# Loading the first slices of weights and of x through one queue in a forced order, in a two-layer hybrid decoder trunk

## The chip, the cores and the metric

The kernel runs on one core of one Trainium2 chip. The metric is the device time of one execution in microseconds; for the kernel before it is the median of three runs. The engines are named as in the profile: PE multiplies matrices (PEld is its weight load), DVE, ACT and POOL are the vector, scalar and GpSimd engines, SP only issues transfers here. ACT has a transfer queue of its own too (ACTq beside SPq in the rows).

## The reference

Two layers, each of them one projection of x (512 tokens by 1024) to 3352 columns, three mixers on slices of those columns, an output projection, and a layer norm:

```python
def hybrid_layer(x, w_in, w_out, ...):
    proj = x @ w_in
    (rq, rk, rv, rg, nq, nkc, nvc, nks, nvs, nkw, nvw, ng, ngl, lx, lg) = jnp.split(proj, IN_SPLIT_POINTS, axis=-1)
    y_ret = retention(rq, rk, rv) * jax.nn.silu(rg)
    y_nsa = nsa(nq, nkc, nvc, nks, nvs, nkw, nvw, ngl, cmp_pos, cmp_w) * jax.nn.silu(ng)
    y_lru = rg_lru(lx, conv_w, conv_b, w_a, b_a, w_x, b_x, lam) * jax.nn.silu(lg)
    y = jnp.concatenate([y_ret, y_nsa, y_lru], axis=-1) @ w_out
    return layer_norm(DEEPNORM_ALPHA * x + y, ln_g, ln_b)
```

`retention` is a chunked decayed attention of 4 heads, `nsa` an attention of 8 query heads with a compressed, a selected and a window branch, `rg_lru` a gated linear recurrence behind a short convolution.

## The kernel before

**Products.** The contraction over 1024 is cut into 8 slices of 128, called k0 to k7. Each operand is split into a rounded high part and a low rest (`wh` and `wl` of the weights, `XH` and `XL` of x), and each k takes three products, high by high, high by low and low by high, which add up in one PSUM bank. The banks are A (three: A_96, A_97, A_98 in the rows of the program), S (two: S_99, S_100), and T, M and O (one each).

**Weights.** The columns of w_in come in chunks of 256 (the first, `nv`, has 280), in the order nv, nk, nq0, cmp, nq1 and so on. A chunk is loaded in two halves of four k each (h0 is k0 to k3, h1 is k4 to k7). A half goes from HBM into one of **two** raw buffers `wr` (wr_86, wr_87), ACT rounds it into one of four `wh` (wh_88 to wh_91), and POOL, in some cases DVE, subtracts into one of four `wl` (wl_92 to wl_95). The next half can be fetched into a raw buffer only when its last `wl` piece has been made. Only the chunk nv of the first layer is different: its two halves, and x itself, come in eight transfers each, one for each k (`load_x` issues the one for x). ACT then makes `XH` and DVE `XL`. In the rows x is written to a buffer named Y, since it borrows a stage of that name.

**The first products.** nv takes 96 products of 280 columns (four tiles of 128 tokens, 8 k, three products), two of its tiles in banks A and two in banks S. nk, nq0 and the later chunks take 48 products of 512 columns each. K, Q and Y are what ACT and DVE copy out of the banks for the attention of nk, nq0 and cmp.

**Order.** The code does not run in the order in which it is written. Every call on an engine is recorded as an `Op` in a `Plan`; `schedule` lists all operations by priorities from their costs (with a little seeded noise), forward and backward six times, and `emit` issues them, engine by engine, in the order of their planned starts. The queue of SP is planned in the same way, as an engine. An engine runs its own list in order, so that an instruction that waits holds up those behind it. A change in the first operations can so change the order of everything behind them.

**Zeros.** `WARM = 9` products of a tile of zeros with itself are recorded into bank T ahead of everything; nothing reads them as a result. `COLD` doubles the planned cost of products that are planned before 6.8 us.

Of the kernel before, what the change touches and what calls it, by code (L numbers as in the profile page):

```python
# [115 lines left out]
BANKS = dict(A=3, M=1, S=2, T=1, O=1)  # L116
PBUFS = 7
WARM = 9
W_ACT = 2

NORM = [["AG", "AG", "VV", "VV"], ["AG", "AG", "VV", "VV"]]
LOCKS = True
# [164 lines left out]
class Plan:  # L287
    ENGINES = ("PE", "DVE", "ACT", "POOL", "SP")

    def __init__(self, nc):  # L290
        self.ops, self.cells, self.bias = [], {}, 0.0
        queues = (nc.tensor, nc.vector, nc.scalar, nc.gpsimd, nc.sync)
        self.engines = [Engine(self, e, q) for e, q in zip(self.ENGINES, queues)]

# [16 lines left out]

    def add(self, eng, call, cost, reads, writes, table, lock, dma=False):
        op = Op(eng, call, cost, table, lock and LOCKS, len(self.ops))
        op.dma = dma
        for r in reads:
            q, m = self.touched(r)
            op.after.update(o for o, q2, m2 in r.buf.writes if q & q2 and m & m2)
        for r in writes:
            q, m = self.touched(r)
            op.after.update(o for o, q2, m2 in r.buf.writes + r.buf.reads if q & q2 and m & m2)  # L320
        for r in reads:
            r.buf.reads.append((op, *self.touched(r)))
        for r in writes:
            b, (q, m) = r.buf, self.touched(r)
            b.writes = [w for w in b.writes if w[1] & ~q or w[2] & ~m] + [(op, q, m)]
            b.reads = [w for w in b.reads if w[0] is op or w[1] & ~q or w[2] & ~m]
        op.after.discard(op)
        op.bufs = {r.buf for r in reads + writes}

        op.rows = {}  # L330
        if eng in ("ACT", "DVE") and not dma:
            for kind, refs in (("W", writes[:1]), ("R", reads)):
                for r in refs:
                    ap = r.view(0)
                    op.rows.setdefault((kind, ap.space == PSUM), ap.offset // ap.ap[0][0])
        for b in op.bufs:
            b.users += 1
        for o in op.after:
            o.before.append(op)
        op.bias = self.bias  # L340
        self.ops.append(op)
# [31 lines left out]
    def forward(self, prio):  # L373

        for b in {b for op in self.ops for b in op.bufs}:
            b.pool.next, b.pool.free = 0, [(0.0, s) for s in range(len(b.pool.slots))]
            b.slot, b.last, b.left, b.seen = None, 0.0, b.users, {}
        for op in self.ops:
            op.wait, op.known = len(op.after), 0.0
        ready = {e: [] for e in self.ENGINES}  # L380
        free = dict.fromkeys(self.ENGINES, BEGIN)

        table, ports = "exp", {"POOL": 0.0, "DVE": 0.0}
        rows = {"ACT": {}, "DVE": {}}
        for op in self.ops:
            if not op.wait:
                ready[op.eng].append(op)
        self.order = []

        def place(op):  # L390

            t = 0.0
            for b in op.bufs:
                if b.slot is None:
                    if b.pool.next != b.at or not b.pool.free:
                        return None
                    t = max(t, min(b.pool.free)[0])
                t = max([t] + [end + TURN for e, end in b.seen.items() if e != op.eng])
            return t

        while len(self.order) < len(self.ops):
            best = None
            for e in ("POOL", "PE", "DVE", "ACT", "SP"):
                pick = None
                for op in ready[e]:
                    at = place(op)
                    if at is None:
                        continue
                    t = max(op.known, at, free[e] + self.held(op, rows), ports[e] if op.lock else 0.0)
                    k = (t, prio[op], op.ix)  # L410
                    if pick is None or k < pick[0]:
                        pick = k, op
                if pick and (best is None or pick[0][0] < best[0][0]):
                    best = pick
            t, op = best[0][0], best[1]
            cost = op.cost
            if op.table and op.table != table:
                cost, table = cost + 1280.0, op.table
            if op.eng == "PE" and t < COLD:
                cost *= 2.0  # L420
            if op.rows:
                rows[op.eng].update(op.rows)
            for b in op.bufs:
                if b.slot is None:
                    _, b.slot = spot = min(b.pool.free)
                    b.pool.free.remove(spot)
                    b.pool.next += 1
            op.start, op.end = t, t + cost
            free[op.eng] = op.end
            if op.lock and op.eng == "POOL":  # L430
                ports["DVE"] = op.end - POOL_EARLY
            elif op.lock:
                ports["POOL"] = op.end
            ready[op.eng].remove(op)
            self.order.append(op)
            for b in op.bufs:
                b.last = max(b.last, op.end + self.release(op))
                if b.pool.turns and op.eng != "PE":
                    b.seen[op.eng] = op.end
                b.left -= 1  # L440
                if not b.left:
                    b.pool.free.append((b.last, b.slot))
            for o in op.before:
                o.wait -= 1
                o.known = max(o.known, op.end + self.lag(op, o))
                if not o.wait:
                    ready[o.eng].append(o)
        return max(op.end for op in self.order)
# [51 lines left out]
def hybrid_kernel(ctx: ExitStack, tc: tile.TileContext, xt_d, xn_d, w_in_d, w_out_d, gb_d, cmpw_d, cmpp_d, lruw_d,  # L500
                  lrup_d, const_d, out_d):
    nc = tc.nc
    plan = Plan(nc)
    T, V, A, G, Q = plan.engines
# [58 lines left out]
    def weights(l, name):  # L563
        if (l, name) not in parts:
            cl, cname, src, n = chunks[len(parts)]
            assert (cl, cname) == (l, name), (l, name)
            s3 = src.rearrange("p (k n) -> p k n", k=KT)
            first = len(parts) == 0
            got = {}
            for h in W_HALVES:  # L570
                r = slice(4 * h, 4 * h + 4)
# [2 lines left out]
                lo = sb([P, 4, 280], "wl", WBUFS, F32R)[:, :, :n]  # L574
                if first:

                    for k in range(4):
                        u = slice(k, k + 1)
                        (A if 4 * h + k < W_ACT else Q).dma_start(raw[:, u, :], s3[:, r, :][:, u, :])
                        load_x(slice(4 * h + k, 4 * h + k + 1))  # L580
                        A.activation(hi[:, u], raw[:, u], AF.Copy)
                        (G if k % 2 else V).tensor_sub(lo[:, u], raw[:, u], hi.bitcast(F32)[:, u])
                else:
                    Q.dma_start(raw, s3[:, r, :])
                    for q in range(2):
                        u = slice(2 * q, 2 * q + 2)
                        A.activation(hi[:, u], raw[:, u], AF.Copy)
                        for v in range(2 * q, 2 * q + 2, 2 // W_CUT):
                            u = slice(v, v + 2 // W_CUT)
                            (G if W_ENG[2 * h + q] == "G" else V).tensor_sub(lo[:, u], raw[:, u], hi.bitcast(F32)[:, u])  # L590
                got[h] = (hi, lo)
            parts[(l, name)] = [(got[k // 4][0][:, k % 4, :], got[k // 4][1][:, k % 4, :]) for k in range(KT)]
        return parts[(l, name)]

# [591 lines left out]
```

## Time and profile before

| | us |
|---|---|
| median of 3 runs | 577.59 (577.09 to 577.8) |
| the profiled execution, its own time | 577.81 |
| its span, first to last instruction | 576.0 |
| PE busy | 559.9 (97% of the span) |
| DVE, ACT, POOL busy | 373.8, 331.6, 336.5 |

The profile is that of one execution. Its own time is 1.8 us more than its span, which lies around the first and the last instruction. An engine counts as busy while one of its instructions runs. Spans of PE are modelled at their ends (products overlap), so the distance from start to start says what one product costs.

### The profile page before, as it was taken

What the parts mean: (1) busy time and instruction counts of PE and PEld (TensorE: products, weight loads), DVE (VectorE), ACT (ScalarE), POOL (GpSimd) and SP (SyncE); (2) the same over time, 40 slices, a digit from 0 to 9 for tenths busy, and PEclk for the clock granted to TensorE, in tenths of its full rate; (3) what the DMA queues carried; (4) which work ended last, traced back from release to release, by engine and by line L of the source; (5) the groups of instructions that cost most, each with busy time, mean ns of one, the idle gap of its engine ahead of it and who ended that gap; (6) DMA issues with size and microseconds to landing.
All of it is one profiled execution on the core that took longest, in us unless ns stands there. A gap on an engine that the chain in (4) does not pass through costs nothing.

```text
span 576.0 us, 10627 instructions
## 1 busy us (share of the span) xinstructions
PE 559.9 (97%) x3718; PEld 500.6 (87%) x3718; DVE 373.8 (65%) x1113; ACT 331.6 (58%) x754; POOL 336.5 (58%) x512
## 2 busy tenths in 40 slices
PE   8999999999999999999989999999999999999994
PEld 7877888889998988899978788888988989889993
DVE  5660378898998754632873026877898886356257
ACT  6453578897775635611535238778967564454230
POOL 3753394377956348844763447633898273478442
PEclk8999999999999999999999999999999999999998
DMA  8743233020323036244253434211122122352303
GB/s 280 243 125 93 77 93 91 15 62 1 79 72 92 1 109 184 93 133 133 98 162 90 126 92 112 73 38 38 38 53 62 33 75 54 114 163 75 109 1 146
DMA packets 44789, 53.67 MB, mean 93 GB/s; under 512 B 3008, under 2 KB 37440, under 8 KB 44736
## 3 DMA queue, kind: packets, MB, share of 16 engines
q1 hardware_dynamic: 44448, 52.71, 31.0%
q8 instruction: 29, 0.48, 0.4%
q10 hardware_dynamic: 288, 0.29, 0.2%
q14 instruction: 24, 0.20, 0.1%
HBM read 47.75 MB, written 4.19 MB: 90 GB/s over the span
## 4 chain that ended last, share of the span: by engine, by line
PE 76%; DVE 9%; ACT 7%; DMA 4%; POOL 2%; issue 2%; DVEq 0%; POOLq 0%; ACTq 0%; SPq 0%
PE A L208 52%; PE T L208 6%; PE O L208 6%; PE S L208 5%; PE M L208 5%; DMA wr<-in_w_in_dram 3%; DVE R L208 2%; DVE P L208 2%; ACT P L208 1%; DVE Y L208 1%; ACT wh L208 1%; PE M L239 1%; DMA lp<-in_lrup_dram 1%; ACT pth L208 1%; POOL wl L208 1%
## 5 line engine op out<-in xcount | busy, mean ns | idle before, releaser
L208 POOL TENSOR_TENSOR wl<-wr,wh 128x256 fp32r<-128x256 f32 (+1 forms) x268 | 199.1, 771 | 114.1 <-ACT wh L208 107.2
L208 PE MATMUL A<-wh,XH 128*128 128x256 f32 (+1 forms) x560 | 154.2, 287 | 2.7 <-ACT wh L208 1.6
L208 PE MATMUL A<-wl,XH 128*128 128x256 f32 (+1 forms) x560 | 154.6, 286 | 0.0
L208 PE MATMUL A<-wh,XL 128*128 128x256 f32 (+1 forms) x560 | 153.5, 285 | 0.3 <-DVE XL L208 0.2
L208 ACT ACTIVATE wh<-wr 128x512 fp32r<-128x512 f32 (+2 forms) x140 | 81.7, 614 | 75.8 <-PE A L208 44.9
L208 PEld LDWEIGHTS A<-wh,XH 128*128 128x128 f32 x560 | 103.9, 189 | 6.3 <-ACT wh L208 1.8
L208 PEld LDWEIGHTS A<-wl,XH 128*128 128x128 f32 x560 | 104.7, 189 | 1.9
L208 PEld LDWEIGHTS A<-wh,XL 128*128 128x128 f32 x560 | 103.9, 189 | 2.6 <-DVE XL L208 0.7
L208 PE MATMUL A<-XH,wh 128*128 128x512 f32 x256 | 100.1, 401 | 0.2 <-DVE K L208 0.2
L208 PE MATMUL A<-XH,wl 128*128 128x512 f32 x256 | 100.1, 400 | 0.0
L208 PE MATMUL A<-XL,wh 128*128 128x512 f32 x256 | 99.2, 397 | 0.0
L208 POOL TENSOR_SCALAR P<-P,den,gate 128x256 f32<-128x256 f32 (+3 forms) x96 | 61.2, 651 | 40.8 <-DVE den L208 38.5
L208 ACT ACTIVATE P<-P,nmx 128x512 f32<-128x512 f32 (+3 forms) x128 | 70.8, 555 | 13.0 <-DVE nmx L208 12.7
L208 ACT ACTIVATE pth<-T 128x512 fp32r<-128x512 f32 x80 | 47.7, 596 | 43.6 <-PE T L208 36.6
L208 DVE TENSOR_TENSOR ptl<-T,pth 128x512 fp32r<-128x512 f32 x80 | 54.9, 686 | 22.1 <-ACT pth L208 21.1
L208 DVE CUSTOM_DVE_ANT_0 P<-S,con 128x512 f32<-128x512 f32 (+3 forms) x128 | 59.6, 484 | 12.9 <-PE S L208 7.4
L208 PE MATMUL S<-K,Q 128*128 128x288 f32 (+4 forms) x240 | 59.9, 340 | 0.3 <-DVE nmx L208 0.3
L208 PEld LDWEIGHTS A<-XH,wh 128*128 128x128 f32 x256 | 48.1, 188 | 10.3 <-issue 0.6
L208 PEld LDWEIGHTS A<-XH,wl 128*128 128x128 f32 x256 | 47.9, 188 | 9.6 <-POOL wl L208 0.5
L208 PEld LDWEIGHTS A<-XL,wh 128*128 128x128 f32 x256 | 48.1, 188 | 9.0
L208 PE MATMUL T<-idr,P 128*128 128x128 f32 x320 | 53.9, 275 | 1.9 <-DVE P L208 1.5
L208 PEld LDWEIGHTS T<-idr,P 128*128 128x128 f32 x320 | 38.4, 141 | 9.0 <-DVE P L208 2.0
(157 smaller groups left out, 860.6 us busy)
## 6 DMA issues: line engine op xcount, KB each, us to landing
wr<-in_w_in_dram SPq DMA_DIRECT2D x48, 512.0 KB, 3.8
wr<-in_w_out_dram SPq DMA_DIRECT2D x16, 512.0 KB, 3.8
Y<-in_xt_dram SPq DMA_DIRECT2D x8, 256.0 KB, 4.5
Y<-in_cmpw_dram SPq DMA_DIRECT2D x4, 512.0 KB, 5.9
R<-in_xn_dram SPq DMA_DIRECT2D x8, 256.0 KB, 3.4
P<-in_gb_dram SPq DMA_DIRECT2D x8, 256.0 KB, 3.9
x<-R SPq DMA_DIRECT2D x8, 256.0 KB, 2.1
R<-x SPq DMA_DIRECT2D x8, 256.0 KB, 3.6
```

The lines of the kernel that those rows point to most:

```text
L208: return f(*[at(x) for x in args], **{k: at(v) for k, v in kw.items()})
L239: self.queue.matmul(out.view(), lhsT.view(), rhs.view(), **kw)
```

## The change

Three things change in the code. `W_ACT = 2`, which put the transfers of w for k0 and k1 on ACT's queue, is gone, and all sixteen first transfers go on SP's. `Plan.chained` makes each of these sixteen follow the one recorded before it, so that the planner can't issue them in another order than w k0, x k0, w k1, x k1, and so on; other transfers may still be planned between two of them. The count of zero products stays at nine, but the planner now places all of them ahead of the first real product.

```diff
-W_ACT = 2
...
     def __init__(self, nc):
         self.ops, self.cells, self.bias = [], {}, 0.0
+        self.chained = None
...
     def add(self, eng, call, cost, reads, writes, table, lock, dma=False):
         op = Op(eng, call, cost, table, lock and LOCKS, len(self.ops))
-        op.dma = dma
+        op.dma, op.follows = dma, None
+        if dma and eng == "SP" and self.chained is not None:
+            op.follows = self.chained[-1] if self.chained else None
+            self.chained.append(op)
...
+        waiting = {op.follows for op in self.ops if op.follows}
         while len(self.order) < len(self.ops):
...
                 for op in ready[e]:
+                    if op.follows and op.follows in waiting:
+                        continue
...
             self.order.append(op)
+            waiting.discard(op)
...
                 if first:
+                    plan.chained = plan.chained or []
                     for k in range(4):
                         u = slice(k, k + 1)
-                        (A if 4 * h + k < W_ACT else Q).dma_start(raw[:, u, :], s3[:, r, :][:, u, :])
+                        Q.dma_start(raw[:, u, :], s3[:, r, :][:, u, :])
                         load_x(slice(4 * h + k, 4 * h + k + 1))
...
                 got[h] = (hi, lo)
+            plan.chained = None
```

The whole plan is made anew. PE's order differs in about the first 30% of the program and again in the attention of the second layer, and is the same from there to 70% and at the end. Three places follow.

**The first transfers on SP.** `wr_86` takes w for k0 to k3 (128x280 each), `wr_87` for k4 to k7, `Y_83` takes x (128x512 each), and `128x4x256` is a whole half of the chunk nk. Before (ACT's queue carried two more transfers `wr_86<-in_w_in_dram 128x280`, as ACT's first instructions, k1 ahead of k0):

```order
L208 DMA Y_83<-in_xt_dram 128x512 x2
L208 DMA wr_86<-in_w_in_dram 128x280 x2
L208 DMA Y_83<-in_xt_dram 128x512 x4
L208 DMA wr_87<-in_w_in_dram 128x280
L208 DMA Y_83<-in_xt_dram 128x512
L208 DMA wr_86<-in_w_in_dram 128x4x256
L208 DMA wr_87<-in_w_in_dram 128x280 x3
L208 DMA Y_83<-in_xt_dram 128x512
```

With the change, from x of k2 on (the five transfers ahead of this piece are w k0, x k0, w k1, x k1, w k2):

```order
L207 DMA Y_83<-in_xt_dram 128x512
L207 DMA wr_86<-in_w_in_dram 128x280
L207 DMA Y_83<-in_xt_dram 128x512
L207 DMA wr_87<-in_w_in_dram 128x280
L207 DMA Y_83<-in_xt_dram 128x512
L207 DMA wr_87<-in_w_in_dram 128x280
L207 DMA Y_83<-in_xt_dram 128x512
L207 DMA wr_87<-in_w_in_dram 128x280
L207 DMA Y_83<-in_xt_dram 128x512
L207 DMA wr_86<-in_w_in_dram 128x4x256
L207 DMA wr_87<-in_w_in_dram 128x280
L207 DMA Y_83<-in_xt_dram 128x512
```

One w and one x now alternate on one queue, and the first half of nk still stands ahead of the last pair.

**PE where nk.h1 and nq0 are first used.** `wh_91` here holds nk.h1 (k4 to k7), `wh_88` then nq0.h0, `wh_89` still k4 to k7 of nv. Before, PE's first product with nk.h1 comes after 88 products of nv and 12 of nk.h0; eight products of nv stand later, right ahead of the first one with nq0.h0 (the last three of the eight here, in S_100):

```order
L208 MATMUL S_100<-wh_89,XH_81 128x280
L208 MATMUL S_100<-wl_93,XH_81 128x280
L208 MATMUL S_100<-wh_89,XL_82 128x280
L208 MATMUL A_97<-XH_81,wh_88 128x512
L208 MATMUL A_97<-XL_82,wh_88 128x512
L208 MATMUL A_97<-XH_81,wl_92 128x512
```

With the change all 96 products of nv and 12 of nk.h0 stand ahead of this piece:

```order
L207 MATMUL A_98<-XH_81,wh_91 128x512
L207 MATMUL A_96<-XH_81,wh_91 128x512
L207 MATMUL A_96<-XL_82,wh_91 128x512
L207 MATMUL A_98<-XL_82,wh_91 128x512
L207 MATMUL A_98<-XH_81,wl_95 128x512
L207 MATMUL A_98<-XH_81,wh_91 128x512
L207 MATMUL A_96<-XH_81,wl_95 128x512
L207 MATMUL A_97<-XH_81,wh_88 128x512
L207 MATMUL A_97<-XL_82,wh_88 128x512
```

The first product with nq0.h0 stands 7 products behind the first with nk.h1 now; before it was the 49th product of 512 columns and is now the 20th. The same stretch of POOL, which makes the low parts, has one more piece of nv (`wl_93<-wr_87,wh_89 128x280`) ahead of the four of nk.h0 (`wl_94<-wr_86,wh_90 128x256`), which free the raw buffer for nk.h1.

**ACT and PE at the end of cmp and nq0.** `Y` and `Q` on ACT's list are copies out of the banks of cmp and nq0. Before, on ACT:

```order
L208 ACTIVATE wh_89<-wr_86 128x2x256 x2
L208 ACTIVATE Y_83<-A_96 64x512 x2
L208 ACTIVATE wh_91<-wr_87 128x2x256 x2
L208 ACTIVATE wh_89<-wr_86 128x2x256
L208 ACTIVATE Y_83<-A_96 64x512
L208 ACTIVATE wh_89<-wr_86 128x2x256
L208 ACTIVATE Q_114<-A_97 64x512
L208 ACTIVATE Y_83<-A_96 64x512
L208 ACTIVATE Q_114<-A_97 64x512
```

With the change, on ACT:

```order
L207 ACTIVATE Y_83<-A_96 64x512
L207 ACTIVATE Y_83<-A_97 64x512
L207 ACTIVATE wh_91<-wr_86 128x2x256 x2
L207 ACTIVATE Q_114<-A_98 64x512
L207 ACTIVATE Y_83<-A_96 64x512
L207 ACTIVATE Y_83<-A_97 64x512
L207 ACTIVATE Q_114<-A_98 64x512
L207 ACTIVATE wh_89<-wr_87 128x2x256 x2
```

and with the change on PE, at the place where A_98 gets its last product and the chunk after it begins in A_96:

```order
L207 MATMUL A_98<-XH_81,wh_89 128x512
L207 MATMUL A_98<-XL_82,wh_89 128x512
L207 MATMUL A_98<-XH_81,wl_93 128x512
L207 MATMUL A_96<-XH_81,wh_88 128x512
L207 MATMUL A_96<-XL_82,wh_88 128x512
```

The copy of Y out of A_96 that frees the bank for `A_96<-XH_81,wh_88` stands behind a copy of Q out of A_98, whose sum PE completes only one row ahead of that product (six products go into A_98 after the last one into A_97 and A_96); before, the copies of A_96 and A_97 were not behind such a copy of another bank.

## Rows read from the trace of the kernel before

**Rows 1.** Windows: length; busy us (and instructions) per engine; granted clock of PE.
```profile
core 0: us, PE busy (x) PEld busy (x) DVE busy (x) ACT busy (x) POOL busy (x), PEclk, DMA share, GB/s
1.04:4.05 3.01, 3.01 (x14) 3.01 (x15) 0.36 (x2) 1.28 (x1) 1.21 (x5) 1.00 0.72 197
4.05:4.51 0.46, 0.46 (x4) 0.27 (x3) 0.00 (x0) 0.00 (x0) 0.00 (x0) 1.00 1.06 394
...
6.16:7.46 1.30, 1.30 (x8) 1.15 (x9) 1.30 (x4) 1.30 (x4) 0.43 (x1) 1.00 1.01 348
7.46:10.87 3.41, 3.41 (x17) 3.41 (x16) 3.41 (x6) 2.66 (x6) 0.72 (x1) 0.50 0.88 269
...
16.00:60.00 44.00, 43.80 (x248) 36.29 (x249) 20.21 (x50) 19.82 (x41) 24.25 (x38) 1.00 0.51 150
60.00:200.00 140.00, 139.53 (x932) 124.86 (x929) 115.67 (x405) 106.73 (x263) 85.60 (x137) 1.00 0.21 56
...
410.00:460.00 50.00, 48.11 (x358) 44.43 (x357) 45.15 (x160) 35.17 (x97) 35.81 (x60) 1.00 0.18 52
```

**Rows 2.** PE's waits over the whole span, summed by releaser: us, times, longest.
```profile
PE A L208 <- ACT wh L208: 1.6, 1, 1.6
...
PE A L208 <- DVE K L208: 0.2, 1, 0.2
```

**Rows 3.** PE's timeline: start, us, what, count, and idle time before it with its releaser.
```profile
1.04 3.47 PE L208 MATMUL T<-kz 128*128 128x128 f32 x16 [1.04 <-DVE kz L208]
6.16 0.53 PE L208 MATMUL A<-wh,XH 128*128 128x280 f32 x2 [1.65 <-ACT wh L208]
...
6.65 0.38 PE L208 MATMUL T<-kz 128*128 128x128 f32 x2
...
12.10 0.29 PE L208 MATMUL A<-wh,XH 128*128 128x280 f32 x1
12.23 0.29 PE L208 MATMUL A<-wl,XH 128*128 128x280 f32 x1
...
22.35 0.39 PE L208 MATMUL A<-XH,wh 128*128 128x512 f32 x1
22.58 0.39 PE L208 MATMUL A<-XL,wh 128*128 128x512 f32 x1
...
31.72 0.39 PE L208 MATMUL A<-XH,wh 128*128 128x512 f32 x1
```

**Rows 4.** SP's timeline of transfer issues; a long entry of several holds waits between them.
```profile
0.72 0.86 SPq L208 DMA_DIRECT2D Y<-in_xt_dram  x2
...
2.57 2.96 SPq L208 DMA_DIRECT2D Y<-in_xt_dram  x4
...
8.56 1.88 SPq L208 DMA_DIRECT2D wr<-in_w_in_dram  x4
...
16.15 2.32 SPq L208 DMA_DIRECT2D wr<-in_w_in_dram  x2
```

**Rows 5.** The tile wr in the first 22 us: time from issue to landing.
```profile
DMA to landing us min/median/max: 3.6/4.3/6.9
```

**Rows 6.** x's stage (tile Y) in the first 22 us: ACT's high parts (ns), and landing.
```profile
L208 ACT ACTIVATE XH<-Y x8: 612/626/632, 5.1 to 14.9; 128x512 fp32r<-128x512 f32 x8
...
DMA to landing us min/median/max: 3.8/4.5/7.6
```

**Rows 7.** The chain that ended last, in order of time: start, us, what.
```profile
0.72 3.99 DMA wr<-in_w_in_dram
...
8.56 3.80 DMA wr<-in_w_in_dram
...
18.09 6.86 DMA wr<-in_w_in_dram
```

**Rows 8.** POOL's timeline: the first six low parts after nk.h0 landed.
```profile
13.09 4.98 POOL L208 TENSOR_TENSOR wl<-wr,wh 128x256 fp32r<-128x256 f32 x6 [4.91 <-ACT wh L208]
```

**Rows 9.** ACT's timeline: the high parts of a half, and two copies of Y.
```profile
20.92 1.15 ACT L208 ACTIVATE wh<-wr 128x512 fp32r<-128x512 f32 x2 [0.23 <-DMA wr<-in_w_in_dram]
...
44.00 1.20 ACT L208 ACTIVATE Y<-A 64x512 f32<-64x512 f32 x2 [5.50 <-PE A L208]
```

**Rows 10.** PE and DVE in the attention of layer 2, about 441 us.
```profile
440.82 2.45 DVE L208 TENSOR_SCALAR P<-P,den,gate 128x128 f32<-128x128 f32 x1
...
443.33 0.33 PE L208 MATMUL T<-idr,P 128*128 128x128 f32 x1 [1.34 <-DVE P L208]
```

## The prediction

> **What bounds the kernel now.** I read the windows first. PE is the bound: over 60 to 200 us it idles less than half a microsecond of 140, over 16 to 60 us 0.2 of 44 [rows 1]. So a faster transfer, rounding or copy is worth only the wait of PE that it ends, and a later one costs only what it makes PE wait. The places where PE now loses time, ahead of 60 us, are few. In the table of waits the longest is one of 1.6 us for a `wh`, the next in this part 0.2 us for K [rows 2]. PE's timeline puts the first at the start: PE runs zeros from 1.04 to 4.51 and begins real products at 6.16 us [rows 3]. The windows show a third loss, which is no wait: from 7.46 to 10.87 the granted clock is 0.50, with 17 products in 3.41 us [rows 1]. The zeros too run at half rate up to 4.05 (14 records in 3.01 us, then 4 in 0.46), whatever the clock's column says ahead of the first event it knows. So PE had sped up at 4.05, stood still for 1.65 us, and was slowed at 7.46, then sped up again at 10.87.
>
> **The start.** SP takes 0.43 us an issue [rows 4]. Before, x k0 went out first at 0.72; now w k0 goes at 0.72 and x k0 at about 1.17. Of the eight transfers of x the shortest took 3.8 us to land, the median 4.5 [rows 6]. The first w, on an empty queue, took 3.99 [rows 7], so I take the short end: 1.17 + 3.8 = 4.97, ACT's `XH` 0.63 [rows 6], first real product at 5.65 (6.35 by the median). Against 6.16 that gives **−0.5** (−0.5 to +0.2). In the row of before PE waited for `wh` and not for x: ACT issued w k1 ahead of k0 and rounded k1 first, which is now gone.
>
> The ninth zero product cost 0.2 to 0.34 of PE's time between real ones (two records from 6.65 [rows 3]); now it lies in the idle time before the first: **−0.3**.
>
> **The clock.** With nine zeros PE works until about 4.75 (two more records at 0.115 us, the rate of the row from 4.05 [rows 1]) and stands still for 0.9 us instead of 1.65. I take it that the clock then stays at its full level. The 3.41 us at half the clock hold work for 1.7: **−1.7** (0 if it falls as before). The Trainium skill (TensorE: Matmul & The Clock Gate, Part 1: The HAM clock gate) says that the gate doesn't start to count with the kernel, so that the moment at which it decides varies from run to run; by that, the same idle time could cost a half-clock stretch in one run and none in another, and a run of before without one would be 1.7 us shorter. The three runs of before lie within 0.71 us of each other, which doesn't show such a run.
>
> **Feeding the first eight k.** A pair of w and x costs SP 0.9 us to issue, nine products of three tiles take PE 9 x 0.128 = 1.15 (start to start, 12.10 and 12.23 [rows 3]). So k0 to k3 come about as fast as PE takes them; the later ones hold the risk that SP sits until an earlier transfer has landed, as in the four issues that took 2.96 us [rows 4]. Small waits in sum **+0.3** (0 to 0.9). Before, the products at half clock left time for it.
>
> **The weights of nk and nq0.** Where PE gains 2.5 us, the weights behind must come 2.5 us earlier, and they don't.
> - nk.h0 goes into the buffer of k0 to k3 when their last low part is made. w k3 is now the seventh transfer of the queue, before it was third. I take the issue at 8.9 instead of 8.56 [rows 4]; landing after 3.8 [rows 7], 12.7.
> - POOL began the low parts 0.73 after nk.h0's landing (8.56 + 3.80 = 12.36, then 13.09), and took 4.98 / 6 = 0.83 for each [rows 7, 8]; the fourth freed the buffer for nk.h1, issued at 16.15 [rows 4]. With 12.7 and the piece of nv that now stands ahead on POOL, which costs nothing to 0.83 according to when k5 arrives, nk.h1 goes at 16.5 to 17.3: taken 16.7. Landing at the median 4.3 [rows 5]: 21.0. ACT's first `wh` is half of 1.15 [rows 9], so it is ready at 21.6 or so.
> - PE gets there after 96 products of nv and 12 of nk: 5.65 + 96 x 0.128 + 12 x 0.232 + 0.3 = 21.0 (0.232 from 22.35 and 22.58 [rows 3]). Before, 88 and 12 sufficed and the product came at 22.35. Wait **+0.65** (0 to 1.2).
> - nq0.h0 goes out when POOL has the last piece of nv, at 18.09 before [rows 7]. The same six pieces stand there; I take 17.5. It took 6.86 us before [rows 7], the longest of all; the median is 4.3 [rows 5]. I take 5.5: landed 23.0, rounded 23.6. PE gets there 7 products after nk.h1, at 21.65 + 7 x 0.232 = 23.3; before, it was at 31.72 [rows 3], since 49 products of 512 columns stood ahead and now 20, so that 6.86 us were hidden. Wait **+0.4** (0 to 1.7).
>
> Every wait here shrinks by what the one ahead of it grows, so that the sum is surer than its parts.
>
> **The banks.** With A_98 taken right after nv, PE waits for ACT to copy K out of it, with a `wh` ahead on ACT: 0.5 instead of the 0.2 of [rows 2], **+0.3** (0 to 0.8). At the end of cmp and nq0 the first product into A_96 needs the copy of Y, which stands on ACT behind the copy of Q out of A_98, and that waits for PE's last product there, one row ahead. A product ends 0.39 us after its start and the next could start at 0.232; each copy takes 1.20 / 2 = 0.60 [rows 3, 9]. So PE waits 0.39 − 0.23 + 2 x 0.60 + some 0.1 to pass it on: **+1.5** (0.76 if the copy of Q doesn't stand ahead, 1.6 at most). Behind PE's product stand all its others, so nothing hides it.
>
> **Behind 60 us.** The window to 200 holds 0.5 us of idle time, of which the new order may lose or gain a little: **−0.1**. In layer 2's attention PE idles 1.9 us of 50 [rows 1]; 1.34 of it is one wait for a DVE step that took 2.45 us with POOL at work beside it [rows 10]. The new order may meet that again, lose it or double it: **0**, with −1.3 to +1.3. What is in the same order, I leave as it is.
>
> **Sum.** −0.5 − 0.3 − 1.7 + 0.3 + 0.65 + 0.4 + 0.3 + 1.5 − 0.1 = +0.55 us on the profiled execution's 577.81 (576.0 of span and 1.8 around it). That execution lies 0.22 above the median of 577.59, which the forecast is compared with: **578.1**. A difference of 0.2% (1.15 us) is about what runs of this kernel can tell from none, so I forecast no change, with 576.9 to 579.2 for this case alone.
>
> **The rivals.**
> *The gain stays* (faster). The weights of nk and nq0 come in time and the copies don't hold PE: nk.h1 lands in the shortest 3.6 [rows 5] and nq0.h0 in 4.3, so that both waits vanish (−1.05), and the copy of Y costs half (−0.75). Then 578.1 − 1.8 = **576.3**, or 575 if the wait of 1.34 us in layer 2 goes too. For it: PE's other waits behind 16 us are so few that the plan as a rule gets its copies in time. Against it: the six products on A_98 leave ACT no other order. Chance 0.30.
>
> *nq0.h0 is as slow as before* (slower). One transfer, 6.86 us again: 17.5 + 6.86 = 24.4, rounded 25.0, while PE is there at 23.3: 1.7 instead of 0.4, **579.4**. A landing at 23.0 is in my sum; from 23.7 on it takes the time over the bound, and each tenth later costs a tenth. For it: it goes out close behind nk.h1 as before. Against it: the other landings are near 4.3. Chance 0.14.
>
> *The clock falls all the same.* The 1.7 us come back, and with them PE is late enough that it waits for neither nk.h1 nor nq0.h0 (1.05): 578.1 + 0.65 = **578.75**. For it: 0.9 us of idle time are still there, and the waits among k0 to k7 add to them. Against it: half as much idle time as before. This is also what the rule of the clock gate would give in some of the runs. Chance 0.20, half of it over the bound.
>
> **Chances.** My forecast 0.36, of which 0.05 lie above the bound through layer 2. Faster 0.30; slower 0.14 + 0.10 + 0.05 = 0.29; within 0.2% the other 0.41. The range goes from below the gain that stays, 575.7, to 579.7, above the slow transfer; outside lie the cases with two of these together, or 1.3 us more or less in layer 2.
>
> **What would show it.** In the trace after: the first real product at 5.5 to 5.8; no stretch at a clock of 0.50 behind it; nk.h1 issued at 16.5 to 17.3 and PE waiting for ACT's `wh` at two places between 20 and 25 us; one wait of 1.4 to 1.6 us of PE for ACT's Y between 50 and 60 us. I am wrong about the start if the product waits for x beyond 6.1, about the clock if its column shows 0.50, and about the sum if the wait for Y is missing, or if layer 2's idle time differs from 1.9 us by over one.

## The result: slower by 0.6%, and the profile after

The changed kernel took 580.9 us (median of 4 runs, 580.01 to 581.86), the kernel before beside it 577.62: a ratio of 1.0059, interval 1.0041 to 1.0076. A second comparison of the same pair gave 1.0064 (1.0047 to 1.0081). The forecast was 578.1 with a range of 575.7 to 579.7, so the kernel is slower by 3.3 to 3.7 us where no change was forecast, and outside the range.

The windows of the changed kernel, to be read beside [rows 1] (length; busy us and count of each engine; granted clock):

```profile
core 0: us, PE busy (x) PEld busy (x) DVE busy (x) ACT busy (x) POOL busy (x), PEclk, DMA share, GB/s
1.04:4.90 3.86, 3.86 (x18) 3.86 (x19) 1.00 (x4) 2.25 (x4) 1.21 (x5) 1.00 0.78 211
4.90:6.88 1.98, 1.98 (x10) 1.98 (x10) 0.76 (x2) 1.10 (x3) 0.88 (x1) 1.00 0.90 288
6.88:16.00 9.12, 8.99 (x69) 8.68 (x67) 5.03 (x9) 6.05 (x14) 2.75 (x4) 1.00 0.99 340
16.00:24.00 8.00, 6.77 (x40) 5.56 (x39) 5.77 (x22) 4.54 (x15) 5.67 (x11) 1.00 0.85 290
24.00:60.00 36.00, 33.49 (x144) 26.47 (x143) 14.17 (x31) 17.98 (x32) 22.75 (x33) 1.00 0.45 119
60.00:200.00 140.00, 138.51 (x957) 123.55 (x956) 111.98 (x391) 101.48 (x253) 81.58 (x132) 1.00 0.20 57
...
410.00:460.00 50.00, 49.22 (x367) 45.47 (x366) 43.96 (x167) 38.75 (x102) 38.97 (x67) 1.00 0.20 54
```

PE's timeline, its first rows and then each row with idle time ahead of it up to 62 us:

```profile
1.04 4.21 PE L207 MATMUL T<-kz 128*128 128x128 f32 x18 [1.04 <-DVE kz L207]
4.90 0.58 PE L207 MATMUL A<-wh,XH 128*128 128x280 f32 x1
...
19.29 0.40 PE L207 MATMUL A<-wl,XH 128*128 128x280 f32 x1 [0.67 <-POOL wl L207]
23.07 0.74 PE L207 MATMUL A<-XH,wh 128*128 128x512 f32 x2 [0.57 <-ACT wh L207]
38.36 0.50 PE L207 MATMUL A<-XH,wh 128*128 128x512 f32 x1 [1.07 <-DVE K L207]
56.80 0.50 PE L207 MATMUL A<-XH,wh 128*128 128x512 f32 x1 [1.44 <-ACT Y L207]
61.30 0.39 PE L238 MATMUL M<-Y 128*64 128x65 f32 x2 [0.74 <-issue]
```

The first real product stands at 4.90 instead of 6.16 [rows 3], a gain of 1.26. Then come five waits of 4.5 us in sum, where before idled 0.2 of 44 us between 16 and 60 [rows 1] (a second profile of before, further down, has one wait of 1.2 us there). The one at 61.30 is put down to "issue"; the products read what two transfers `Y<-Y` bring, which SP issued from 56.77 on, right behind the copies of Y that PE had waited for at 56.80. In the attention of layer 2 PE idled 0.8 us of 50, against 1.9 [rows 1]: the wait of 1.34 us of [rows 10] isn't there.

SP's issues in the changed kernel, beside [rows 4] (start, us, what):

```profile
0.72 0.38 SPq L207 DMA_DIRECT2D wr<-in_w_in_dram  x1
1.16 0.42 SPq L207 DMA_DIRECT2D Y<-in_xt_dram  x1
...
9.15 0.93 SPq L207 DMA_DIRECT2D wr<-in_w_in_dram  x2
...
18.53 1.11 SPq L207 DMA_DIRECT2D wr<-in_w_in_dram  x2
```

And the chain that ended last, three of its pieces up to 22.4 us (start, us, what):

```profile
9.15 5.31 DMA wr<-in_w_in_dram
...
16.59 1.93 POOL wl L207 x2
...
18.53 3.83 DMA wr<-in_w_in_dram
```

nk.h0 went out at 9.15 and took 5.31 us to land, not 3.80 [rows 7]; so POOL's low parts were done at 18.5 and nk.h1 went out there, not at 16.15 [rows 4]. In the change the way up to 24 us is that of nk.h0, POOL's low parts and nk.h1.

### The profile page after: what moved, and what is told of

Same layout as the page of the kernel before. It is cut to its first block, busy times and chain, and to the rows that moved or that the text cites. A ratio compares the mean times of both kernels' runs of the same rounds, so it can differ in the third digit from the quotient of the medians.

```text
span 579.2 us, 10616 instructions
## 1 busy us (share of the span) xinstructions
PE 560.5 (97%) x3718; PEld 500.0 (86%) x3718; DVE 370.4 (64%) x1113; ACT 331.9 (57%) x754; POOL 336.1 (58%) x512
## 4 chain that ended last, share of the span: by engine, by line
PE 74%; DVE 6%; POOL 6%; DMA 6%; ACT 5%; issue 2%; SPq 0%; DVEq 0%; POOLq 0%; ACTq 0%
PE A L207 51%; PE T L207 6%; PE O L207 6%; PE S L207 5%; PE M L207 4%; DMA wr<-in_w_in_dram 4%; POOL wl L207 4%; DVE R L207 1%; POOL P L207 1%; PE M L238 1%; ACT wh L207 1%; ACT P L207 1%; DMA wr<-in_w_out_dram 1%; DVE P L207 1%; DMA Y<-in_xt_dram 1%
## 5 line engine op out<-in xcount | busy, mean ns | idle before, releaser
L207 ACT ACTIVATE P<-P,nmx 128x384 f32<-128x384 f32 (+3 forms) x128 | 70.8, 555 | 13.6 <-DVE nmx L207 12.9
L207 DVE CUSTOM_DVE_ANT_0 P<-S,con 128x384 f32<-128x384 f32 (+3 forms) x128 | 59.7, 482 | 11.9 <-PE S L207 8.7
L207 PE MATMUL S<-K,Q 128*128 128x288 f32 (+4 forms) x240 | 58.5, 339 | 0.5 <-DVE nmx L207 0.5
```

The lines of the kernel that those rows point to most:

```text
L207: return f(*[at(x) for x in args], **{k: at(v) for k, v in kw.items()})
```

## The experiments

The kernels are compared by their ratio to before in the same comparison, since the median of before itself lay between 576.67 and 577.46 in them (100 runs). "Place of 24 us" is worked out from each trace: the time at which PE begins the first product ahead of which it has done at least as many columns of real products (the zeros left out, in order) as before had at 24.19 us in the profile shown ahead. The places of 12, 18 us and so on are meant in the same way. "By hand" means that the plan was made as it was, and then single operations were put elsewhere in one engine's list.

| run | us | ratio (interval) | place of 24 us | first real product |
|---|---|---|---|---|
| before, profile ahead | 577.59 | | 24.19 | 6.16 |
| before again | 576.80 | 0.9991 (0.9974 to 1.0008) | 24.35 | 5.80 |
| before, ninth zero ahead | 576.32 | 0.9981 (0.9962 to 0.9999) | 24.52 | 5.69 |
| the change | 580.90 | 1.0059 (1.0041 to 1.0076) | 24.11 | 4.90 |
| the change again | 581.01 | 1.0064 (1.0047 to 1.0081) | 23.86 | 4.90 |
| change, 14 zeros | 579.95 | 1.0052 (1.0036 to 1.0068) | 24.47 | 6.05 |
| change, two queues | 580.35 | 1.0050 (1.0032 to 1.0069) | 24.26 | 5.06 |
| old order, new loads | 578.12 | 1.0027 (1.0014 to 1.0040) | 24.71 | 4.90 |
| new order, old loads | 585.53 | 1.0140 (1.0110 to 1.0171) | 28.89 | 5.74 |
| change, K first | 579.11 | 1.0047 (1.0033 to 1.0061) | 23.55 | 4.89 |
| change, Y first | 580.86 | 1.0079 (1.0053 to 1.0105) | 25.06 | 4.90 |
| change, four places | 579.49 | 1.0055 (1.0033 to 1.0076) | 24.52 | 4.90 |
| change, K, Y and Y to Y | 578.17 | 1.0020 (0.9996 to 1.0044) | 24.21 | 4.89 |
| old order, own buffer | 577.54 | 1.0002 (0.9983 to 1.0021) | 25.45 | 4.90 |
| ... and supply free | 577.83 | 1.0009 (0.9994 to 1.0024) | 26.31 | 4.90 |
| ... and two queues | 576.66 | 0.9989 (0.9975 to 1.0003) | 23.41 | 5.10 |
| ... and k7 first | 576.02 | 0.9978 (0.9963 to 0.9993) | 22.79 | 5.60 |
| before, seed 11 | 603.52 | 1.0449 (1.0404 to 1.0493) | | 5.35 |
| change, seed 11 | 600.54 | 1.0379 (1.0334 to 1.0424) | | 4.90 |

### Is the first product on the path?

The old order with the change's loads, by hand:

```diff
 SP:  +w k0, x k0, w k1, x k1, ... x k6, nk.h0, w k7, x k7 (all sixteen, as in the change), the rest as before
 ACT: -two transfers of w     +wh and XH of k0, k1, k2 ... in turn
 DVE, POOL: +XL and wl of the eight k in turn
 PE:  +the ninth zero product ahead of the first real one, the rest as before
```

> The order of the kernel before, with only the start of the change put into it by hand: the sixteen first transfers on SP in the forced order (nk.h0 ahead of the last pair, as in the changed kernel), ACT, DVE and POOL taking the eight k in turn, and the ninth zero product ahead of the first real one. Theory A (the new order of everything behind the start costs the time, and the start itself gains some 2 us): first real product near 4.9 us, PE then 2 us ahead of before, of which up to 0.7 is lost where nk.h1 has 0.8 to 1.1 us to spare: 575.4 to 576.5. Theory B (the loads themselves cost it: PE runs into weights that one queue can't bring sooner): 577.6 or slower, with waits for ACT's wh or POOL's wl between 12 and 25 us of 2 us or more in sum.

Neither theory had it whole. The start gains as the change's does, PE is 2 us ahead at the place of 12 us, and is 0.5 us *behind* the profile of before at that of 24. The waits on the way are small (the longest 0.81 for POOL's `wl` at 18.5, 0.23 for `wh` at 22.7), but they take the whole gain back. By its ratio of 1.0027 this kernel is some 1.6 us slower than before, so the loads, put in by hand in this way, cost something in the old order too; the profile is behind by 0.4 to 0.5 us at the place of 24 and 0.8 at its end, and where the rest goes isn't shown.

Five zeros more in the change, so that PE begins later:

```diff
-zero product 8: once
+zero product 8: six times
```

> The changed kernel with five zero products more, fourteen in all, ahead of the first real one, which so comes 1 to 2 us later. Theory (the start of PE is off the path, since the weights of nk decide when PE passes 24 us): the product that the change reaches at 24.1 us is reached at 24.0 to 24.5 all the same, and the time is that of the change, 580.4 to 581.4. Rival (the start is on the path): 1 to 2 us later there and at the end, 582 to 583.

PE's timeline in that run:

```profile
1.04 5.26 PE L207 MATMUL T<-kz 128*128 128x128 f32 x28 [1.04 <-DVE kz L207]
6.05 0.38 PE L207 MATMUL A<-wh,XH 128*128 128x280 f32 x1
...
23.43 0.74 PE L207 MATMUL A<-XH,wh 128*128 128x512 f32 x2 [1.13 <-ACT wh L207]
38.43 0.50 PE L207 MATMUL A<-XH,wh 128*128 128x512 f32 x1 [0.76 <-DVE K L207]
```

The real products begin 1.15 us later, but at the place of 12 us only 0.41 of that is left (10.13 against 9.72), since the first ten products run slowly in the change and not here. So the delay tested is 0.4 us and not 1.15. At the place of 18 it is gone (16.36 against 16.35); the wait for POOL's `wl` behind it is 0.21 instead of 0.67. At 24 PE is 0.36 behind the change and 0.61 behind its second run, with a longer wait for nk.h1, and nothing of it is in the time (1.0052 against 1.0059 and 1.0064). That a later start is swallowed is shown for this small delay; the two profiles of before, next, show it for a larger one.

Before once more, unchanged:

> The kernel before, unchanged, against itself: a second profile of it and what a ratio shows where there is no change. Theory of the clock (the stretch at half clock from 7.46 to 10.87 us in the first profile of before comes and goes from run to run): this profile has none, and PE passes the place of 10.87 us about 1.7 us earlier, but the place of 24.19 us within 0.4 us of the first profile. Rival: the stretch is there again, since the idle time of 1.65 us ahead of the first real product is.

Its windows (columns as above) were:

```profile
5.80:7.46 1.66, 1.66 (x11) 1.60 (x12) 1.66 (x4) 1.43 (x4) 0.79 (x1) 1.00 1.02 379
7.46:10.87 3.41, 3.38 (x27) 3.16 (x25) 3.41 (x7) 3.18 (x6) 0.24 (x1) 1.00 0.95 318
...
16.00:24.00 8.00, 6.77 (x41) 5.87 (x40) 3.98 (x20) 3.47 (x11) 5.54 (x11) 1.00 0.81 249
```

And of PE's timeline in that run the first real product and the one wait on the way:

```profile
5.80 0.53 PE L208 MATMUL A<-wh,XH 128*128 128x280 f32 x2 [0.99 <-ACT wh L208]
...
17.70 0.39 PE L208 MATMUL A<-wl,XH 128*128 128x280 f32 x1 [1.23 <-POOL wl L208]
```

The stretch at half clock (1.2 of 2.4 GHz) isn't there: 27 products between 7.46 and 10.87, at a clock of 1.00, instead of 17 at 0.50 [rows 1]. PE comes to the place of 12 us 1.9 us sooner, and then waits for POOL, 1.23 us at 17.70, and in sum 1.2 of 8 us between 16 and 24, so that it passes the place of 24 us 0.16 *later*. So the stretch comes and goes in one and the same code, and in this place it cost nothing: without it PE waits for POOL's last low part of nv, which stands behind those of nk.h0. The Trainium skill (TensorE: Matmul & The Clock Gate, Part 1: The HAM clock gate) says that the gate's count isn't tied to the start of the kernel, and so the moment of its decision varies from run to run; these two profiles of before agree, one with 3.41 us at half clock and one with none. Of the 100 runs of before, one has a mean granted clock of 0.992 as the profile ahead had, and three have 0.994, the others more. How many of them had such a stretch isn't known: a profile further down (the supply free, one queue) has one of 3.41 us at a mean of 0.994. The run at 0.992 took 579.51 us, 2.6 more than the median of its comparison, and what its clock had to do with that no profile shows.

The ninth zero alone, by hand:

> The kernel before with one thing of the change: the ninth zero product ahead of the first real one, all else in the order of before. By the prediction's term: 0.2 to 0.34 us faster. Rival: nothing, since the first weights of nk end the time that PE wins here, as they did in the run with the old order and the new start.

0.9981 (0.9962 to 0.9999) is more than the 0.3 us of the forecast and only just excludes nothing; before again, with no edit at all, gave 0.9991. Its profile has the wait for POOL's `wl` too, 1.55 us at 18.10, and passes the place of 24 us at 24.52, later than before.

### The order or the loads?

The fourth corner, the change with its loads undone by hand:

> The changed kernel with only its loads undone by hand: two of w on ACT's queue, the rest of the sixteen on SP in the order of before, and ACT, DVE and POOL taking the first eight k in that order; all else in the order of the change, nine zeros ahead. It is the fourth corner beside before (old order, old loads: 576.9 in these comparisons), the old order with the new loads (578.1) and the change (580.9). Theory (the order of all else is what costs, the loads hardly matter): 580.0 to 581.2, with the waits for K near 38 us and for Y near 57 us as in the change. Rival (the loads cost it): 577 to 578.5.

It came out on neither side: 585.5, slower than both parents. PE waits 2.56 us for a `wl` of nv that its new order wants early and the old loads bring late, and then runs at half clock. A row of PE's timeline:

```profile
17.26 0.83 PE L208 MATMUL A<-wl,XH 128*128 128x280 f32 x2 [2.56 <-POOL wl L208]
```

And a row of the windows (columns as above):

```profile
16.89:20.30 3.41, 3.04 (x13) 3.04 (x14) 1.24 (x4) 0.83 (x2) 2.56 (x7) 0.50 0.79 226
```

Here no wait behind the stretch hides it: PE has no other wait of note up to that for K's copy at 43.13, and passes the place of 24 us at 28.89. The waits for K, Y and Y to Y follow as in the change (1.06, 1.44, 0.74). All four runs have a mean granted clock of 0.990 to 0.994. So there is no cost of the order and one of the loads that add up. By the ratios the new order is slower than the old by 1.8 to 2.1 us with the new loads (1.0059 and 1.0064 against 1.0027), and by 8.1 with the old.

The change with two of w on ACT's queue, k0 ahead, and the change once more beside it:

> The changed kernel with the first two of w on ACT's queue once more (k0 ahead of k1, x of k0 and k1 first on SP), everything else in the order of the change. With the supply free, one queue was 1.2 us slower than two. Theory (the forced order on one queue costs of itself, since the second x comes late and SP's later transfers wait for it): 579.3 to 580.4. Rival (in the change the weights of nk hold PE whatever the loads do): 580.9, and 24.1 us is passed at the same time.

> The changed kernel, unchanged, beside the others on the same chip: 580.4 to 581.4 if the first comparison was sound, with the waits for K near 38 us, for Y near 57 and for the transfers Y to Y behind it again. If the waits are gone, they were chance.

1.0050 against 1.0064, with intervals that overlap: not told apart, and the place of 24 us is no sooner (24.26, 23.86). With two queues nk.h1 went out at 16.89 instead of 18.53, and landed at 22.51 instead of 22.36: PE waits 1.87 us for it and for nothing ahead of it. The second profile of the change has all five waits again (0.67, 0.32, 1.13, 1.44 and 0.74 us), so they belong to this plan and not to one run.

### The waits behind 24 us

The copies of K out of A_98 by hand, on ACT:

```diff
+K<-A_98 (first)
 wh, first half of nq0.h1
-K<-A_98 (first)
 wh, second half of nq0.h1
+K<-A_98 (second)
 K<-K
-K<-A_98 (second)
```

> The changed kernel, with only the two copies of K out of A_98 moved on ACT, the first ahead of the weights of nq0.h1 for whose landing ACT stands idle, the second ahead of a copy of K to K. Theory A: the wait of 1.07 us near 38 us goes: 579.8 (579.4 to 580.3). Rival: PE takes the time back waiting for Y near 57 us, since ACT's list there is as long as before: 580.9.

The copies of Y, on ACT:

```diff
+Y<-A_96, Y<-A_97 (second halves)
 wh_91<-wr_86 x2
 Q<-A_98
-Y<-A_96, Y<-A_97 (second halves)
```

On SP, in the run with K, Y and Y to Y:

```diff
+Y<-Y x2
 wr_87<-in_w_in_dram
-Y<-Y x2
```

> The changed kernel, with only the copies of Y out of A_96 and A_97 moved on ACT, ahead of the weights and the copy of Q that stand before them. Theory A (those copies hold PE, and the two transfers Y to Y behind them): both waits, 1.44 and 0.74 us, go: 578.7 (578.2 to 579.5). Rival: the weights that ACT now makes 1.1 us later hold PE in their place: 580.3 or more.

> The changed kernel, with four of its places put in another order by hand: on ACT the copies of Y out of A_96 and A_97 ahead of the weights and of the copy of Q; on ACT the copies of K out of A_98 ahead of the weights and copies that wait for nq0.h1 or for DVE; on SP, ACT and POOL the last pair of nv ahead of nk.h0. Theory A: the waits of 0.67, 1.07, 1.44 and 0.74 us go, 580.9 - 3.9 = 577.0 (576.4 to 578). Theory B: the waits come back at the next product that needs weights; 579.5 or more.

> The changed kernel with K's copies moved as in the run that gained 1.8 us, Y's copies moved as in the run that gained nothing, and the two transfers Y to Y moved ahead of the half of weights that stands before them on SP. Theory: the copies of Y were only one half of the chain, the other was that SP waits for a raw buffer ahead of the transfers Y to Y; with both moved, the waits of 1.4 and 0.7 to 1.6 us near 55 to 60 us go: 579.1 - 2.2 = 576.9 (576.3 to 577.8). Rival: the weights behind those transfers hold PE instead: 578.5 or more.

Why K's copy is late in the change, ACT's timeline shows:

```profile
33.71 0.63 ACT L207 ACTIVATE wh<-wr 128x512 fp32r<-128x512 f32 x1 [1.11 <-DMA wr<-in_w_in_dram]
34.25 0.58 ACT L207 ACTIVATE K<-A 64x512 fp32r<-64x512 f32 x1
```

ACT stands idle 1.11 us for the landing of nq0.h1, with the copy of K behind it in its list. With K first the wait of 1.07 us at 38.36 is gone from PE's timeline, and the one for Y stays, as long as before and 1.9 us earlier:

```profile
22.52 0.73 PE L207 MATMUL A<-XH,wh 128*128 128x512 f32 x2 [0.42 <-ACT wh L207]
54.91 0.50 PE L207 MATMUL A<-XH,wh 128*128 128x512 f32 x1 [1.45 <-ACT Y L207]
```

With only Y first the wait for Y is gone, and PE waits for the transfers `Y<-Y` instead. SP's issues in that run:

```profile
55.48 0.37 SPq L207 DMA_DIRECT2D wr<-in_w_in_dram  x1
56.35 1.35 SPq L207 DMA_DIRECT2D Y<-Y  x2
```

And PE's product that reads them:

```profile
61.68 0.39 PE L240 MATMUL M<-Y 128*64 128x65 f32 x2 [1.55 <-issue]
```

The time from issue to landing of the two `Y<-Y`, in the change, with only Y first, and with K, Y and Y to Y moved:

```profile
DMA to landing us min/median/max: 3.1/3.4/3.7
DMA to landing us min/median/max: 4.1/4.3/4.5
DMA to landing us min/median/max: 3.1/3.4/3.6
```

The last expectation above says that SP, waiting for a raw buffer, held these transfers back. The rows say otherwise: `Y<-Y` went out at 56.35, right behind the copy of Y that ended at 56.33. But it now stood 0.87 us behind a half of weights, and took 4.1 and 4.5 us to land, so that the wait went from 0.74 to 1.55 us. Two other waits of that profile were longer too (1.95 for `wh` at 24.04, 1.21 for K at 39.46), and the time didn't fall at all. The run with four places moved has the same wait for `Y<-Y` (1.54) and the same landings (4.3 and 4.5), and isn't better than K alone. With `Y<-Y` ahead of that half of weights it lands in 3.1 and 3.6 us again. Its wait is then the one that is left:

```profile
58.48 0.39 PE L240 MATMUL M<-Y 128*64 128x65 f32 x2 [0.69 <-issue]
```

Only with K, Y and `Y<-Y` moved together does the loss shrink to 1.0020 (0.9996 to 1.0044; two of these ten runs took 581.4 and 581.7 us). Of some 3.5 us, 0.7 to 1.0 was K (1.0059 and 1.0064 to 1.0047) and 1.6 the chain of Y (1.0047 to 1.0020); each of the two is a difference of ratios with intervals of 0.15 to 0.25%. (The 1.8 us that an expectation gives K compares medians of two comparisons.) The traces agree: between 24 and 62 us PE is busy 34.75 of 38 us in the change, 35.84 with K moved and 37.31 with all three.

### What holds PE up to 24 us

nk.h0 into an idle buffer, so that it waits for no low part:

```diff
-nk.h0 -> wr_86 (when k0 to k3 are done with)
+nk.h0 -> lt, nk.h1 -> wr_86, both right behind the sixteen
```

> The run with the order of before and the new start, once more, with one thing more: nk.h0 goes into an idle buffer of the recurrence's (lt) and not into the raw buffer of k0 to k3, and nk.h0 and nk.h1 are issued right behind the sixteen first transfers. Theory B1 (the two raw buffers hold the weights of nk back, and so eat the earlier start): the waits at 18.5 and 22.7 us go, 578.12 - 1.4 = 576.7 or less, faster than before by up to 1. Theory B2 (the transfers as a whole do, since the 16 DMA engines are busy all the time until 16 us): no better than 577.8, and x and w of k4 to k7 come no sooner.

1.0002 (to 1.0021) against 1.0027 (from 1.0014): inconclusive, and the place of 24 us comes later (25.45). PE now waited for x of k1 (1.04 us at 6.84), for nk.h0 itself (0.89 at 15.66) and for a `wl` (0.81 at 19.78).

The constants and all that belongs to them out of the way too, first on one queue:

```diff
 SP:   16 transfers, nk.h0, nk.h1, +nq0.h0,  con, R, lruw, lp, cmpw, -nq0.h0
 ACT:  +wh of nk.h1,  vst and gate copies,  -wh of nk.h1, idr and lwh behind the weights
 POOL: lwl behind the weights of nq0    DVE: the steps on lp behind K's
```

Then the same on two queues:

```diff
-SP: w k0, x k0, w k1, x k1, w k2, ...
+ACT: w k0, w k1      SP: x k0, x k1, w k2, x k2, w k3, ...
```

> The order of before with the new start and nk.h0 in the idle buffer of the recurrence's, as in the run with its own buffer, and now all that is not needed before 30 us out of the way of the weights: nq0.h0 right behind nk.h1 on SP and the constants (con, R, lruw, lp, cmpw) behind it; ACT's high parts of nk.h1 ahead of the first copies out of the banks, ACT's idr and lwh, POOL's lwl and DVE's chain of small steps on lp behind the weights of nk and nq0. Theory (the supply of the weights of nk decides when PE passes 24 us, the first product doesn't): the product that every version so far reaches at 24.1 to 25.5 us is reached 1 to 2 us sooner, and the time is 574.8 to 576.2, if the copies of K and Y keep up. Rival (the 16 DMA engines, busy until 16 us whatever is first, bind): 24 us or later there, and 576.5 to 578.

> The same, with the first two of w on ACT's queue again, k0 ahead of k1, and x of k0 and k1 first on SP. Theory: the second pair lands up to half a microsecond sooner (two queues issue it), so the wait for x of k1 near 7 us shrinks; 0 to 0.5 us faster than the same kernel on one queue. Rival: the transfers share the same engines, so that no pair comes sooner: the same time.

> The version of two queues and an own buffer for nk.h0, in the order of before, with one place more mended: ACT, POOL and DVE make k7's high and low parts of nv ahead of those of nk.h0, for which PE waited 0.98 us at 17.8. Theory (the supply holds PE up to 24 us, piece by piece): 0.5 to 1 us less, 575.7 to 576.2, and now clear of before, a ratio of 0.997 to 0.9985. Rival: the low parts of nk.h0, later by 0.8, hold PE in their place: as before, 576.7.

On one queue the theory failed: 26.31 us at that place, and 1.0009. SP's issues in that run:

```profile
5.42 0.74 SPq L209 DMA_DIRECT2D wr<-in_w_in_dram  x1
7.01 0.33 SPq L209 DMA_DIRECT2D Y<-in_xt_dram  x1
```

And PE's wait for the second x:

```profile
7.70 0.39 PE L209 MATMUL A<-wh,XH 128*128 128x280 f32 x1 [1.53 <-ACT XH L209]
```

x of k1, the fourth transfer, issued at 2.10, landed at 6.99, and SP issued nothing between 6.2 and 7.0: its next transfer began when that one had landed. That profile also has the stretch at half clock (9.15 to 12.57), which makes its place of 24 us later. On two queues x of k1 was there at 4.8, no wait of PE ahead of 17.7 us is over 0.2, and the place of 24 us comes at 23.41. The time, 576.66 against 577.83, is 1.2 us less, with intervals of the ratios that still overlap. With k7's parts ahead of nk.h0's as well, PE's wait at 17.76 (0.81, for a `wl`) goes and it passes the place at 22.79, 1.4 to 1.7 us before the three versions of before; the time is 0.9978 of before (0.9963 to 0.9993), 576.02 us: faster than both kernels, by about as much as PE is ahead there.

### Another draw of the plan

`SEED = 11` for 12, in the change and in before:

> The changed kernel with SEED = 11 in place of 12: the same loads in the same forced order, another order of all else. Theory A2 (what the change cost is for the most part the luck of one plan): another time by a microsecond or more either way, 578 to 584, with other waits behind 25 us, and the same ones ahead of it. Theory B (the forced loads cost it): 580 to 582, with the same waits ahead of 25 us making up most of it.

> The kernel before with SEED = 11 in place of 12: the same operations and loads, only other noise in the priorities. The changed kernel with this seed took 600.5 us. Theory (what a new plan costs is its own luck, the kernel's seed is a good draw and other draws are worse by many microseconds whatever the loads are): 585 to 605. Rival (before's plans are steadier, the forced chain makes plans bad): 576 to 582.

600.5 and 603.5 us: neither side of the first expectation had so much, and the second was written with the first result known. The seed alone moves before by 26 us and the change by 20, and at seed 11 the change isn't the slower of the two (their intervals overlap). Part of this is the clock: the two profiles have 13.7 us (the change) and 20.5 us (before) at half clock ahead of their last stretch. So at that seed it isn't the forced chain that makes the plan slow, and the 3.5 us at seed 12 are small beside what one other seed did; no third seed was run.

## Why the prediction was wrong, step by step

Three terms failed. Of the gain ahead of 24 us (the start, the ninth zero, the clock) the sum kept 1.15 us, and 0.08 was left. K's wait was put at 0.5 us and took 1.07. The wait for the transfers `Y<-Y`, 0.74, was put at nothing.

- **The start** was right in sign and too small: 4.90 us, not 5.65. The first w landed 2.3 us after its issue and the first x 2.9, less than any row ahead had (3.6 and 3.8, [rows 5, 6]). But the gain is worth nothing behind 24 us (24.11 against 24.19).
- **The clock is the step that failed first.** −1.7 rested on one profile. Before again shows no such stretch and is no faster for it: PE is 1.9 us ahead at the place of 12 us, waits for POOL, and is 0.16 behind at 24. The forecast did ask whether before has runs without the stretch, and took the 0.71 us between its three runs for a no; but a run without it isn't shorter, so that this spread can't tell. The sign asked for (no stretch at 0.50 in the change) came true and was worth nothing. The change's own profile pays at its start: its last zero ends at 5.25 us, not 4.75, and the first ten real products run slowly, up to 6.88 us (10 products in 1.98 us).
- **The weights of nk and nq0.** The forecast gave back 1.35 us of 2.5 up to here (0.3 + 0.65 + 0.4). All but 0.08 was given back (24.11 against 24.19): in the change the place of 24 us is set by nk.h0, POOL's low parts and nk.h1. nk.h1 went out at 18.53, not 16.7, for the most part because nk.h0 took 5.31 us to land. An earlier issue alone doesn't mend it: with two queues nk.h1 went out at 16.89 and landed no sooner. I had seen that the weights don't come earlier, and still let 1.15 us of the gain through. nq0.h0 held nothing: it went out at 19.27 and landed 4.5 later, in time since PE was late, so that the rival on it failed. A wait of 0.67 for a `wl` of nv at 19.3, behind nk.h0's on POOL, wasn't in the sum.
- **The banks.** Y was right: 1.5 forecast, 1.44 measured. K was mis-sized: 1.07 and not 0.5, since the copy of K stood on ACT behind the first half of nq0.h1, which ACT had to wait for. Missing was what is late next behind Y: SP's transfers `Y<-Y` and the products on them, 0.74.
- **Behind 60 us** −0.1 was about right: from 62 to 460 us PE is busy 393.57 of 398, before 393.31. The wait of 1.34 us of [rows 10] is missing in the change's profile, but also in that of before again, whose busy time there is the same all the same (393.43): this wait comes and goes without the total moving with it. By the forecast's own sign, layer 2's idle time off by over one (0.8 for 1.9), the sum should have moved.
- **The sum** of +0.55, with 1.07 more at the weights (−0.08 where −1.15 stood), 0.57 more at K, 0.74 at Y to Y and 0.06 less at Y, is 2.9. The trace has it so: between 24 and 62 us PE is busy 34.75 of 38 us, before 37.80, which is 3.05 lost in one place; the spans differ by 579.2 − 576.0 = 3.2, the kernels by 3.4 to 3.7 (from the ratios). Of the rivals each was of the size of one wait; none said that the whole gain ahead of 24 us is off the path.

Left open: why the fourth transfer, the second x, took 4.9 us in one run with one queue and 3.3 in another, whether one queue costs the change itself anything (1.0050 against 1.0064 doesn't tell), and why nk.h0 and nk.h1 take longer to land in some runs. The five waits come back in a second profile of this plan; that another plan of the changed code would not have them is supported by the seeds, not shown.

## What to carry to other kernels

A gain at the start counts only as far as the next thing that doesn't move with it: follow the chain of transfers, rounding and buffers up to the first place where all versions meet, and test it by starting later on purpose, reading from the trace how much later the real work then is. A stretch of low clock, or a long wait, in one profile of a kernel is a sample; look at the clock of its other runs before counting on it. When an order is planned anew, waits between copies out of banks and the transfers behind them can cost more than what was changed gains. Read them as pairs (the copy, and the transfer that waits for it), since mending one of a pair moved the wait here and gained nothing.

## What the runs showed of the chip

The half-clock stretch of the kernel before (7.46 to 10.87 us) is in its first profile and not in its second. One of the same length behind a wait of 2.56 us, in the new order with the old loads, stood where nothing hid it. The first transfer landed 2.1 to 2.3 us after its issue in eleven profiles with one queue issuing; with two, the first w took 3.3 to 4.0 and the first x 3.1 to 3.8 us in eight. x of k1 took 3.3 to 4.9 us in the eleven with one queue (in the change 3.84), and 3.6 to 4.2 in the eight with two, where it went out 0.9 us sooner. The first wait for `P` in layer 2 (1.34 us) and one for `R` near 292 us (0.6 or 1.6 us) differ between the two profiles of before.
